# One core, two layers: the even layer's output projection in one pass over eight depth blocks, with the gated unit's results kept in DRAM

## The chip, the cores and the metric

One core of a Trainium2 chip runs the whole program. The time is device microseconds from the start to the end of one execution; three executions of the kernel before were timed, and one more was profiled.

TensorE multiplies (PE in the profile, its weight loads PEld), VectorE (DVE), ScalarE (ACT) and GpSimd (POOL) work on tiles, and SyncE (SP) issues every transfer of this kernel. TensorE's granted clock has two levels, 1.2 and 2.4 GHz; the profile's 1.00 is the higher.

## The reference, cut to what matters

2176 tokens (128 of a prompt, 2048 of a sample) of width 1024 in float32 pass two layers. The even layer has two branches of width 512 behind one input projection: a gated linear recurrence in two directions (o_a), and a state space model whose result passes a gated unit (o_b2). Both go through one output projection and are added to the residual. The odd layer is a gated short convolution with its own projections. What the change touches is this:

```python
    y = jax.nn.gelu(y.reshape(bsz, L, B_WIDTH))
    y = y * jax.nn.sigmoid(jnp.dot(y, w_glu) + b_glu)
...
    o_a = o.reshape(bsz, L, A_WIDTH) * jax.nn.silu(g_a)
...
    o_b2 = y_b * jax.nn.silu(g_b)
    out = jnp.dot(jnp.concatenate([o_a, o_b2], axis=-1).astype(h.dtype), w_out)
...
        yp = (yp.astype(F32) + g_p[:, None, :] * op.astype(F32)).astype(x_prompt.dtype)
        ys = (ys.astype(F32) + g_s[:, None, :] * os_.astype(F32)).astype(x_sample.dtype)
```

The depth of the output projection is 1024, which is eight blocks of 128: blocks 0 to 3 are o_a, blocks 4 to 7 are o_b2.

## The kernel before, in words

**Layout.** Features lie on the 128 partitions and tokens along them. The tokens are cut into six tiles (`TILES`): five of 384 and a last one, tile 5, of 256; `PARTS` makes pairs 0 (tiles 0, 1), 1 (2, 3) and 2 (4, 5). A float32 factor is split into hi and lo of type float32r, and a product is three matmuls, hi with hi, hi with lo, lo with hi (`mm3`, L356). A tile of activations split so is an `hhi` and an `hlo` of [128, 8, 384] from the pool `hp`, which has three slots for each of the two names.

**The order.** The tile framework orders the instructions of each engine ahead of time, by priority (in the main the order in which the program states them) and by its own model of time; on the chip each engine then runs its list in order, and waits where something is late. SP's list of transfers is such a list too: a transfer that waits holds up those behind it.

**The stages around the change.** First come the input projections, the scan of the state space model (its gelu results go to `y_d`) and the forward scan of the recurrence (`hgrn_run`), all interleaved. Gates go to DRAM as `zga` and `zgb`. Then:

- `bwd_chunk` (L891) does the backward scan, one chunk of 128 tokens after the other from chunk 16 down to 0. It loads `op_d`, `zga`, `qb_d` and `kv_d` (256 KB each), adds the backward part, normalises (a root on ScalarE, L922), transposes and stores 256 KB of o_a to `o_d` (L931). Chunks 16 to 12 are pair 2's tokens.
- `glu` (L949) works on a pair. It loads y into an `hlo` slot (L960), makes hi and lo copies for each tile in an `hhi` slot (L970, L971), and for each of four blocks does 12 matmuls (L979), a sigmoid out of PSUM (L983), the product with the gate `zgb` on GpSimd (L984), that with y on VectorE (L985), and a split into hi and lo (L986). y is stored with the 8 phases of a token group apart, so L970, L971 and L985 read it element by element. The results of the two tiles lie packed in one `hhi` and one `hlo` slot.
- `out_second` (L1000) multiplies these, blocks 4 to 7, by their half of the weights, 12 matmuls per output block and tile, and adds the result to x on VectorE (`evac_out`, L996). For pairs 0 and 1 the half-finished residual is stored to `x_d` (L1013); pair 2's stays in SBUF.
- The main loop then takes the pairs 2, 1, 0, with the later tile of each first (5, 4, then 3, 2, then 1, 0). `out_pair` with l = 0 multiplies blocks 0 to 3, which `load_o` (L1283) has read from `o_d` and split, by the other half of the weights, four output blocks at a time (`OUTE`), and adds; squares are summed on the way for the norm. Then come the backward chunks of the next pair, the odd layer's input projection and convolution (`in_odd`), the loads for the next pair, and `out_pair` with l = 1, two output blocks at a time, whose end normalises and stores the output.

**Buffers.** `big` is one slot of [128, 8, 384] that raw loads of `load_o` and the second tile's convolution results share. `xr` has three slots for residuals, `zg` four for the gates, `st` four for sigmoids. PSUM gives the gated unit two banks for matmul results, and the main loop five. Weights (512 KB a load) are split by ScalarE (L342) and by VectorE or GpSimd in turn (L346).

## Time and profile before

| | us |
|---|---|
| median of three runs | 2485.75 |
| lowest and highest | 2468.01, 2489.28 |
| the profiled execution | 2480.67 |
| its span, first to last instruction | 2478.9 |

The profile is of one execution. Busy time is the time in which an engine has an instruction; matmuls overlap each other, so the mean of one (some 330 ns) is longer than its share of the time. Idle time before an instruction is put down to what released it last. In the windows PEclk is the mean granted clock, DMA the mean busy share of 16 transfer engines; it can pass 1 a little where transfers overlap the edge of a window.

### The profile page before, as it was taken

What the parts mean: (1) busy time and instruction counts of PE and PEld (TensorE: products, weight loads), DVE (VectorE), ACT (ScalarE), POOL (GpSimd) and SP (SyncE); (2) the same over time, 40 slices, a digit from 0 to 9 for tenths busy, and PEclk for the clock granted to TensorE, in tenths of its full rate; (3) what the DMA queues carried; (4) which work ended last, traced back from release to release, by engine and by line L of the source; (5) the groups of instructions that cost most, each with busy time, mean ns of one, the idle gap of its engine ahead of it and who ended that gap; (6) DMA issues with size and microseconds to landing.
All of it is one profiled execution on the core that took longest, in us unless ns stands there. A gap on an engine that the chain in (4) does not pass through costs nothing. (4 is left out here: it accounts for less than half of the span.)

```text
span 2478.9 us, 46614 instructions
## 1 busy us (share of the span) xinstructions
PE 2320.4 (94%) x18452; PEld 2224.6 (90%) x18452; DVE 1381.5 (56%) x2960; ACT 988.5 (40%) x1989; POOL 678.1 (27%) x740
## 2 busy tenths in 40 slices
PE   5999889999999889998988899999999999999997
PEld 3999788988988779987988899999999999899997
DVE  5976879755557883366777632255622245522233
ACT  3544322334466774465444332233422232422231
POOL 0233431323223233233122222223222222322221
PEclk8999989999999899999998999999999999999999
DMA  7576643555575474554876332234221224122121
GB/s 261 148 221 198 195 138 101 152 149 149 150 219 161 133 220 133 170 160 126 295 252 213 111 95 76 77 102 158 72 64 60 68 78 139 57 64 65 60 68 60
DMA packets 277418, 335.96 MB, mean 136 GB/s; under 512 B 79056, under 2 KB 221136, under 8 KB 277072
## 3 DMA queue, kind: packets, MB, share of 16 engines
q1 hardware_dynamic: 277200, 332.99, 43.4%
q8 instruction: 145, 2.38, 0.4%
q14 instruction: 73, 0.60, 0.1%
HBM read 260.98 MB, written 71.94 MB: 134 GB/s over the span
## 5 line engine op out<-in xcount | busy, mean ns | idle before, releaser
L362 PE MATMUL pj<-hhi,whi 128*128 128x384 f32 (+1 forms) x3648 | 1173.5, 332 | 43.3 <-ACT hhi L304 25.9
L362 PE MATMUL pj<-hlo,whi 128*128 128x384 f32 (+1 forms) x3648 | 1174.9, 331 | 7.5 <-DVE hlo L305 5.8
L362 PE MATMUL pj<-hhi,wlo 128*128 128x384 f32 (+1 forms) x3456 | 1139.8, 330 | 0.1
L362 PEld LDWEIGHTS pj<-hhi,whi 128*128 128x128 f32 x3648 | 688.3, 190 | 55.0 <-ACT hhi L304 27.8
L362 PEld LDWEIGHTS pj<-hlo,whi 128*128 128x128 f32 x3648 | 688.4, 190 | 13.8 <-DVE hlo L305 8.5
L362 PEld LDWEIGHTS pj<-hhi,wlo 128*128 128x128 f32 x3456 | 657.9, 190 | 1.8 <-POOL wlo L346 0.6
L346 POOL TENSOR_TENSOR wlo<-wraw,whi 128x256 fp32r<-128x256 f32 x472 | 378.2, 832 | 1013.3 <-ACT whi L342 971.5
L342 ACT ACTIVATE whi<-wraw 128x512 fp32r<-128x512 f32 x472 | 271.7, 623 | 563.9 <-PE pj L362 358.1
L346 DVE TENSOR_TENSOR wlo<-wraw,whi 128x256 fp32r<-128x256 f32 x472 | 186.2, 452 | 114.2 <-ACT whi L342 113.3
L1056 DVE TENSOR_TENSOR ccg<-ccg,pj 128x384 f32<-128x384 f32 (+1 forms) x48 | 25.5, 531 | 248.2 <-PE pj L362 232.5
L829 POOL TENSOR_TENSOR hK<-hK,ht 128x512 f32<-128x512 f32 x68 | 93.3, 1373 | 242.7 <-ACT hMg L813 160.0
L996 DVE SCALAR_TENSOR_TENSOR xr<-pj,mod,xr 128x384 f32<-128x384 f32 (+2 forms) x152 | 77.4, 530 | 135.3 <-PE pj L362 123.2
L304 ACT ACTIVATE hhi<-nsq,mod 128x384 fp32r<-128x384 f32 (+2 forms) x144 | 74.3, 557 | 56.0 <-DVE nsq L302 55.9
L831 DVE TENSOR_TENSOR hQ<-hQ,ht 128x512 f32<-128x512 f32 x102 | 82.5, 822 | 15.4 <-PE lv L799 11.4
L283 DVE TENSOR_TENSOR nac<-nac,nsq 128x384 f32<-128x384 f32 (+1 forms) x112 | 72.3, 646 | 29.5 <-ACT nsq L282 27.4
L305 DVE SCALAR_TENSOR_TENSOR hlo<-nsq,mod,hhi 128x384 fp32r<-128x384 f32 (+2 forms) x144 | 82.0, 597 | 2.6 <-ACT hhi L304 2.6
L282 ACT ACTIVATE nsq<-xr 128x384 f32<-128x384 f32 (+1 forms) x84 | 42.0, 503 | 97.1 <-DVE xr L996 92.0
L1076 DVE TENSOR_TENSOR ccs<-ccs,pj 128x384 f32<-128x384 f32 (+1 forms) x48 | 25.3, 527 | 89.2 <-ACT ccs L1075 89.2
L572 POOL TENSOR_TENSOR SOt<-C,L 128x544 f32<-128x544 f32 x32 | 38.0, 1186 | 121.9 <-DVE SO L573 117.3
L979 PE MATMUL pj<-hhi 128*128 128x384 f32 (+1 forms) x192 | 54.0, 358 | 18.3 <-ACT hhi L970 12.2
L813 ACT ACTIVATE hMg<-hK 128x512 f32<-128x512 f32 x85 | 55.3, 653 | 37.2 <-PE lv L799 23.9
L1071 DVE TENSOR_TENSOR cca<-cca,pj 128x384 f32<-128x384 f32 (+1 forms) x48 | 25.4, 529 | 79.9 <-PE pj L362 79.7
(299 smaller groups left out, 2831.0 us busy)
## 6 DMA issues: line engine op xcount, KB each, us to landing
wraw<-in_w_in_odd SPq DMA_DIRECT2D x96, 512.0 KB
wraw<-in_w_in_even SPq DMA_DIRECT2D x92, 512.0 KB
mwm<-in_w_mod SPq DMA_DIRECT2D x64, 256.0 KB
big<-in_x SPq DMA_DIRECT2D x10, 1536.0 KB
wraw<-in_w_out_even SPq DMA_DIRECT2D x24, 512.0 KB
wraw<-in_w_out_odd SPq DMA_DIRECT2D x24, 512.0 KB
su<-u_d SPq DMA_DIRECT2D x64, 136.0 KB
pe<-et_d SPq DMA_DIRECT2D x32, 256.0 KB
```

The source lines that it names most:

```text
L282: nc.scalar.activation(sq[:, :n], x, AF.Square)
L283: e.tensor_tensor(acc, acc, sq[:, :n], op=OP.add)
L304: A.activation(hi[:, k, a:b], raw[:, a:b], AF.Identity, bias=sh)
L305: V.scalar_tensor_tensor(lo[:, k, a:b], raw[:, a:b], sh, hi[:, k, a:b].bitcast(F32), op0=OP.add, op1=OP.subtract)
L342: nc.scalar.activation(hi[:, i:i + ca], raw[:, i:i + ca], AF.Copy)
L346: e.tensor_tensor(lo[:, k], raw[:, k], hi[:, k].bitcast(F32), op=OP.subtract)
L362: nc.tensor.matmul(out=P[:, :n], lhsT=a[:, k, :], rhs=b[:, k, :n], start=(k == 0 and i == 0), stop=(k == kd - 1 and i == 2))
L813: A.activation(vw(Mg, 0, [(h, 2), (2 * h, nb), (1, h)]), vw(KK, 0, sp), AF.Copy)
L829: (G if lvl in KPOOL else V).tensor_tensor(kv, kv, vw(tot, n + 1, [(-n - 1, 2), (2, nb), (0, h)]), op=OP.mult)
L831: V.tensor_tensor(qv, qv, vw(tot, 1, [(n - 1, 2), (2, nb), (0, h)]), op=OP.mult)
L979: T.matmul(out=P[:, :n], lhsT=w[:, k, b * 128:b * 128 + 128], rhs=x[:, :n], start=(k == 0 and j == 0), stop=(k == 3 and j == 2))
L996: nc.vector.scalar_tensor_tensor(x[:, a:e], P[:, a:e], g.mod[l][:, 16 + b, s:s + 1], x[:, a:e], op0=OP.mult, op1=OP.add)
```

## The change

- `glu` no longer splits its results and no longer returns them. It takes y in the order in which it is stored, so that L970, L971 and L985 run over whole runs; matmuls and sigmoid see the tokens in that order. The product with y comes first, on VectorE; GpSimd then multiplies into the gate's tile `zgb`, reading the sigmoid's tile element by element to restore the order of the tokens, and that tile is stored to blocks 4 to 7 of `o_d`, which grows from four to eight blocks.
- `out_second`, `load_halves` and `x_d` are gone. The three pairs' gated units stand one after the other.
- `load_o` takes one tile, all eight blocks in one transfer into `big`, and splits it into its own `hhi` and `hlo`. For the first pair both tiles and x are loaded right behind the gated units. In the loop the next pair's first tile is loaded ahead of `out_pair` with l = 1, and its second tile behind it.
- `out_pair` treats both layers alike: eight depth blocks, 24 matmuls per output block and tile, two output blocks at a time (`OUTN`).
- x is read from the input for every pair.

```diff
--- before.py
+++ after.py
@@ -34,7 +34,6 @@
 EPS = 1e-6
 MAGIC = 12582912.0
 NQ = 2
-ORD2 = (0, 1, 2)
 NZG = 4
 RI = 500
 XP = 8
@@ -44,8 +43,7 @@
 AH = 1
 RS = 0
 GB = 8
-OUTE = 4
-OUTO = 2
+OUTN = 2
 NMD = 8
 MWB = 3
 RX = 0
@@ -345,12 +343,6 @@
         k = slice(i, i + cl)
         e.tensor_tensor(lo[:, k], raw[:, k], hi[:, k].bitcast(F32), op=OP.subtract)
     return hi, lo
-
-
-def load_halves(nc, g, src):
-
-    w = load_w(nc, g, src.rearrange("b p k m -> p b k m"))
-    return [tuple(t[:, 4 * i:4 * i + 4] for t in w) for i in range(2)]
 
 
 def mm3(nc, P, n, w, h):
@@ -959,17 +951,15 @@
             c0 = NSAM if s == 0 else (a - SEQ) // 8
             nc.sync.dma_start(rw[:, b, :, o:o + m], g.y_d[b * 128:b * 128 + 128, :, c0:c0 + m])
             o += m
-    out = {}
-    for i, ti in enumerate(pair):
+    for ti in pair:
         n = TILES[ti][1] - TILES[ti][0]
         m, c0 = n // 8, (TILES[ti][0] - t0) // 8
         hl = g.hp.tile([128, KD, 384], F32R, name="hhi")
-        ys = [vw(rw, b * 8 * mc + c0, [(1, m), (mc, 8)]) for b in range(4)]
+        ys = [vw(rw, b * 8 * mc + c0, [(mc, 8), (1, m)]) for b in range(4)]
         for b in range(4):
-            h = vw(hl, b * 384, [(8, m), (1, 8)])
+            h = vw(hl, b * 384, [(m, 8), (1, m)])
             A.activation(h, ys[b], AF.Copy)
-            V.tensor_tensor(vw(hl, (4 + b) * 384, [(8, m), (1, 8)]), ys[b], h.bitcast(F32), op=OP.subtract)
-        ob = g.hp.tile([128, KD, 384], F32R, name=("hhi", "hlo")[i])
+            V.tensor_tensor(vw(hl, (4 + b) * 384, [(m, 8), (1, m)]), ys[b], h.bitcast(F32), op=OP.subtract)
         for b in range(4):
             gb = g.zg.tile([128, 384], F32, name="zgb")
             nc.sync.dma_start(gb[:, :n], g.zgb[b, :, TILES[ti][0]:TILES[ti][1]])
@@ -981,11 +971,10 @@
             sg = g.st.tile([128, 384], F32, name="zst")
             b0 = PV["bglu"][0] + b
             A.activation(sg[:, :n], P[:, :n], AF.Sigmoid, bias=g.pv[:, b0:b0 + 1])
-            G.tensor_tensor(sg[:, :n], sg[:, :n], gb[:, :n], op=OP.mult)
-            V.tensor_tensor(vw(sg, 0, [(8, m), (1, 8)]), vw(sg, 0, [(8, m), (1, 8)]), ys[b], op=OP.mult)
-            split(nc, ob[:, b, :n], ob[:, 4 + b, :n], sg[:, :n])
-        out[ti] = ob[:, 0:4], ob[:, 4:8]
-    return out
+            V.tensor_tensor(vw(sg, 0, [(m, 8), (1, m)]), vw(sg, 0, [(m, 8), (1, m)]), ys[b], op=OP.mult)
+            gv = vw(gb, 0, [(8, m), (1, 8)])
+            G.tensor_tensor(gv, gv, vw(sg, 0, [(1, m), (m, 8)]), op=OP.mult)
+            nc.sync.dma_start(g.o_d[4 + b, :, TILES[ti][0]:TILES[ti][1]], gb[:, :n])
 
 
 
@@ -997,33 +986,13 @@
                                        op0=OP.mult, op1=OP.add)
 
 
-def out_second(nc, g, tiles, hs, xs, store):
-
-    for b in range(KD):
-        if b % 2 == 0:
-            ws = load_halves(nc, g, g.I["w_out_even"][b:b + 2, :, 4:8])
-        w = ws[b % 2]
-        for ti in tiles:
-            t0, t1 = TILES[ti]
-            n = t1 - t0
-            P = next(g.ps_p).tile([128, 512], F32, name="pj")
-            mm3(nc, P, n, w, hs[ti])
-            evac_out(nc, g, 0, ti, b, P, xs[ti][:, b])
-            if store and b % 2:
-                nc.sync.dma_start(g.x_d[(b - 1) * 128:b * 128 + 128, t0:t1].rearrange("(k p) t -> p k t", p=128),
-                                  xs[ti][:, b - 1:b + 1])
-
-
 def out_pair(nc, g, l, tiles, hs, xs, done):
 
     acc = {ti: g.nr.tile([128, 384], F32, name="nac") for ti in tiles}
-    m = (OUTE, OUTO)[l]
-    for b0 in range(0, KD, m):
-        b1 = b0 + m
-        if l == 0:
-            ws = [w for b in range(b0, b1, 2) for w in load_halves(nc, g, g.I["w_out_even"][b:b + 2, :, 0:4])]
-        else:
-            ws = [load_w(nc, g, g.I["w_out_odd"][b]) for b in range(b0, b1)]
+    w_out = g.I[("w_out_even", "w_out_odd")[l]]
+    for b0 in range(0, KD, OUTN):
+        b1 = b0 + OUTN
+        ws = [load_w(nc, g, w_out[b]) for b in range(b0, b1)]
         for ti in tiles:
             n = TILES[ti][1] - TILES[ti][0]
             for b, w in zip(range(b0, b1), ws):
@@ -1100,8 +1069,7 @@
     for nm in ("zq", "zff", "zfb", "zv", "zga", "zgb"):
         setattr(g, nm, dram(nm, [4, 128, NTOK]))
     g.op_d = dram("op_d", [NCH, 128, 512])
-    g.o_d = dram("o_d", [4, 128, NTOK])
-    g.x_d = dram("x_d", [D, NTOK])
+    g.o_d = dram("o_d", [8, 128, NTOK])
     g.h_d = dram("h_d", [6, 128, 2, KD, 384])
     g.u_d = dram("u_d", [512, 8, NC8])
     g.y_d = dram("y_d", [512, 8, NC8])
@@ -1280,25 +1248,18 @@
                     Sb = bwd_chunk(nc, g, c, Sb)
             return Sb
 
-        def load_o(pair):
-            raw = big(g)
-            os = {}
-            for i, ti in enumerate(pair):
-                t0, t1 = TILES[ti]
-                n = t1 - t0
-                r = raw[:, 4 * i:4 * i + 4, :n]
-                nc.sync.dma_start(r, g.o_d[:, :, t0:t1].rearrange("h p t -> p h t"))
-                o = g.hp.tile([128, KD, 384], F32R, name=("hhi", "hlo")[i])
-                for k in range(4):
-                    split(nc, o[:, k, :n], o[:, 4 + k, :n], r[:, k])
-                os[ti] = o[:, 0:4], o[:, 4:8]
-            return os
+        def load_o(ti):
+            t0, t1 = TILES[ti]
+            n = t1 - t0
+            r = big(g)[:, :, :n]
+            nc.sync.dma_start(r, g.o_d[:, :, t0:t1].rearrange("h p t -> p h t"))
+            return split_tile(nc, g, r, n)
 
         def xr():
             return g.xr.tile([128, KD, 384], F32, name="xr")
 
-        def load_xs(pair, src, rooms=None):
-            return {ti: load_x(nc, g, ti, src, rooms[i] if rooms else xr()) for i, ti in enumerate(pair)}
+        def load_xs(pair):
+            return {ti: load_x(nc, g, ti, I["x"], xr()) for ti in pair}
 
         def norm_odd(ti, sq):
             n = TILES[ti][1] - TILES[ti][0]
@@ -1320,13 +1281,11 @@
         order = [p[::-1] for p in (p2, p1, p0)]
         Sb = bwd(p2, Sb)
         with tc.tile_pool(name="zg", bufs=NZG) as g.zg:
-            for pair in ORD2:
-                obs = glu(nc, g, PARTS[pair], wg)
-                last = pair == 2
-                xs = load_xs(PARTS[pair], I["x"], None if last else (xr(), big(g)))
-                out_second(nc, g, PARTS[pair], obs, xs, not last)
+            for pair in PARTS:
+                glu(nc, g, pair, wg)
         g.ps_p, g.wp = itertools.cycle((ps_q, ps_p, ps_q, ps_p, ps_q)), itertools.cycle(((wp2, wp), (wp, wp), (wp, wp)))
-        os = load_o(order[0])
+        os = {ti: load_o(ti) for ti in order[0]}
+        xs = load_xs(order[0])
         for i, pair in enumerate(order):
             ta, tb = pair
             nxt = order[i + 1] if i < 2 else None
@@ -1348,9 +1307,11 @@
             nb = TILES[tb][1] - TILES[tb][0]
             ys = {ta: ya, tb: split_tile(nc, g, yb[:, :, :nb], nb)}
             if nxt:
-                os, xn = load_o(nxt), load_xs(nxt, g.x_d)
+                os = {nxt[0]: load_o(nxt[0])}
+                xn = load_xs(nxt)
             out_pair(nc, g, 1, pair, ys, xs, finish)
             if nxt:
+                os[nxt[1]] = load_o(nxt[1])
                 xs = xn
 
 
```

## Rows read from the trace of the kernel before

**Rows 1.** The page: span, busy time, share of the chain by engine.

```profile
span 2478.9 us, 46614 instructions
...
PE 2320.4 (94%) x18452; PEld 2224.6 (90%) x18452; DVE 1381.5 (56%) x2960; ACT 988.5 (40%) x1989; POOL 678.1 (27%) x740
...
PE 46%; DVE 2%; ACT 1%; issue 0%; POOL 0%; DVEq 0%; POOLq 0%; ACTq 0%
```

**Rows 2.** Windows: start:end, length, busy us (count) PE PEld DVE ACT POOL, PEclk, DMA, GB/s.

```profile
1418.00:1690.00 272.00, 272.00 (x1854) 271.96 (x1855) 103.97 (x225) 86.19 (x171) 70.55 (x92) 1.00 0.28 86
```

**Rows 3.** Windows, columns as above: the touched stretch, cut by stage.

```profile
1158.50:1199.00 40.50, 31.21 (x262) 27.34 (x248) 23.32 (x42) 23.14 (x43) 8.90 (x10) 0.92 0.68 190
1199.00:1236.70 37.70, 36.86 (x216) 35.89 (x217) 26.08 (x55) 12.58 (x18) 4.87 (x6) 1.00 1.06 346
1236.70:1265.00 28.30, 22.32 (x111) 20.62 (x110) 20.36 (x30) 14.99 (x24) 11.92 (x11) 0.88 0.80 276
1265.00:1302.00 37.00, 36.45 (x220) 36.03 (x219) 26.87 (x55) 11.65 (x20) 5.59 (x5) 1.00 0.81 244
1302.00:1325.40 23.40, 19.55 (x120) 19.03 (x119) 16.26 (x32) 14.57 (x25) 8.43 (x11) 0.85 0.97 311
1325.40:1391.00 65.60, 62.49 (x417) 61.32 (x415) 41.92 (x91) 25.32 (x50) 19.29 (x25) 0.95 0.42 133
```

**Rows 4.** Windows of rows 3, projection matmuls (L362) alone: PE and PEld.

```profile
1199.00:1236.70 37.70, 34.75 (x192) 33.08 (x192) 1.00 1.06 346
...
1265.00:1302.00 37.00, 34.40 (x192) 32.87 (x191) 1.00 0.81 244
```

**Rows 5.** Groups by line, 1158.5:1391: form, count, busy, mean ns, idle before and releaser.

```profile
L979 PE MATMUL pj<-hhi 128*128 128x384 f32 (+1 forms) x192 | 54.0, 358 | 18.3 <-ACT hhi L970 12.2 <-ACT zst L983 4.7 <-DVE hhi L971 1.2
...
L996 DVE SCALAR_TENSOR_TENSOR xr<-pj,mod,xr 128x256 f32<-128x256 f32 (+2 forms) x54 | 26.9, 516 | 27.6 <-PE pj L362 27.1
...
L984 POOL TENSOR_TENSOR zst<-zst,zgb 128x384 f32<-128x384 f32 (+1 forms) x24 | 24.6, 1036 | 63.4 <-ACT zst L983 28.1 <-DVE wlo L346 17.0 <-issue 9.7
...
L985 DVE TENSOR_TENSOR zst<-zst,hlo 128x384 f32<-128x384 f32 (+1 forms) x24 | 22.3, 935 | 12.4 <-POOL zst L984 12.4
L971 DVE TENSOR_TENSOR hhi<-hlo,hhi 128x384 fp32r<-128x384 f32 (+1 forms) x24 | 20.4, 876 | 11.0 <-ACT hhi L970 11.0
...
L970 ACT ACTIVATE hhi<-hlo 128x384 fp32r<-128x384 f32 (+1 forms) x24 | 19.1, 842 | 11.8 <-DMA hlo<-y_d 11.8
...
L983 ACT ACTIVATE zst<-pj,pv 128x384 f32<-128x384 f32 (+1 forms) x24 | 13.1, 561 | 19.7 <-PE pj L979 19.4
...
L922 ACT ACT_TABLE_LOAD x7 | 9.0, 1283 | 0.1
```

**Rows 6.** Timeline of ACT, first uses of two loads.

```profile
1164.35 0.85 ACT L970 ACTIVATE hhi<-hlo 128x384 fp32r<-128x384 f32 x1 [6.44 <-DMA hlo<-y_d]
...
1649.17 1.77 ACT L311 ACTIVATE hhi<-big 128x384 fp32r<-128x384 f32 x4 [3.40 <-DMA big<-o_d]
```

**Rows 7.** Timeline of SP's DMA issues: start, length of the issue, line, tiles, count.

```profile
1159.10 1.27 SPq L960 DMA_DIRECT2D hlo<-y_d  x2
...
1295.55 0.36 SPq L931 DMA_DIRECT2D o_d<-bo  x1
...
1345.72 0.37 SPq L931 DMA_DIRECT2D o_d<-bo  x1
...
1348.11 0.33 SPq L897 DMA_DIRECT2D bo<-op_d  x1
...
1643.93 0.93 SPq L1290 DMA_DIRECT2D big<-o_d  x2
```

**Rows 8.** Timeline of PE: start, length, instruction, [idle before and releaser].

```profile
1246.64 0.62 PE L979 MATMUL pj<-hhi 128*128 128x384 f32 x2 [1.44 <-ACT hhi L970]
...
1256.46 1.01 PE L979 MATMUL pj<-hhi 128*128 128x384 f32 x2 [3.98 <-ACT zst L983]
...
1315.01 0.80 PE L979 MATMUL pj<-hhi 128*128 128x256 f32 x2 [3.46 <-ACT hhi L970]
```

## Prediction

> **What bounds the kernel now.** I read the page first: TensorE is busy for 2320.4 of 2478.9 us, and of the chain that ended last, as far as it was followed, TensorE holds 46 of 49 hundredths [rows 1]. So a change that leaves TensorE's instructions alone can give or take only the time in which TensorE idles or runs at its lower clock, and I looked for that time stage by stage. Behind the touched stretch there is next to none: 272 us of the odd layer are 272.00 us busy at granted clock 1.00 [rows 2]. The touched stretch is 1158.5 to 1391 us, and the table of windows [rows 3] holds the whole argument: gated unit of pair 0 with the tail of the forward scan; second half of its projection; the same two for pair 1; gated unit of pair 2; then pair 2's second half and first half together. Idle time is length less PE busy: 9.3, 0.8, 6.0, 0.6, 3.9 and 3.1, together 23.6 us. A stretch at mean clock c has lost (1 - c) of its length, since the low level is half the high one (1.2 against 2.4 GHz): 3.2, 0, 3.4, 0, 3.5, 3.3, together 13.4 us. Before, then, 37.0 of these 232.5 us are lost, and 195.5 are work. The reader should see that the loss sits in the gated unit, not in the projection: the two stretches that are mostly projection lose 1.4 us in 74.7.
>
> **What is moved at no price.** The projection multiplies as before: 24 matmuls per output block and tile, now in one accumulation instead of 12 and 12. 192 matmuls (pair 0) take 34.75 us and pair 1's 34.40 [rows 4]. These 69 us leave the stretch and come back as longer projections of pairs 1 and 0, where TensorE has weights ready in the same rhythm: by the loops one weight load still serves 48 matmuls, 24 loads before and 24 after. So the sum is: new time = old time + (loss after - 37.0).
>
> Also costed at nothing: 56 residual updates (L996, half a microsecond each [rows 5]) go, VectorE being 104 us busy in those 272 [rows 2]; 12.6 MB of residuals (4 tiles of 1.57 MB, stored and reloaded) go, 8.9 MB of gated results written and read come, in stretches where DMA has a share of 0.28 [rows 2]. The splits into hi and lo stay 48 in number; those of the gated half move from the gated unit to the load of the projection's input. For later pairs these lie under the odd projection (about 69 us for two tiles at the pace of [rows 4]): the first tile's load follows the last use of the one raw buffer, the second tile's splits wait for the slot that the odd projection's first tile frees, and have its last 48 matmuls and then the next tile's 48, 8.7 us each, against 8 splits at 0.44 us (four in 1.77 [rows 6]) and as many subtractions. Waiting for that slot, they hold up ScalarE's queue (squares, weight splits), which has this much slack. Were that cover gone, each of two pairs would lose some 5 us.
>
> **Loss after, term by term.**
> (a) The start of the first gated unit: 9.3 + 3.2 = 12.5 us now, mostly a wait for y (issued 1159.10, first copy 1164.35, matmul later [rows 6, 7]). The copies L970 and subtractions L971 now read and write runs instead of single elements; the row for contiguous copies is 0.44 us [rows 6] against 0.84 and 0.88 [rows 5]. I take 11.
>
> (b) Gated units 2 and 3 lose 9.8 + 6.9 = 16.7 us now. Two of their waits are for L970 of a pair's second tile, 1.44 and 3.46 us [rows 8]: of three slots for hi one holds the gate's weights, one the first tile's copies, one its results, so the second tile's copies wait until the first tile's matmuls end. The change takes the results out of these slots. That returns 4.9 us and one fall of the clock, 3.5. The other wait, 3.98 us for the sigmoid [rows 8], comes from a backward scan chunk on ScalarE: its root needs another table than the sigmoid, 1.28 us each way [rows 5], while two PSUM buffers hold 4.2 us of matmuls. Three gated units now run without a projection between them, so the five chunks of pair 2 fall into them: I add 2.7. Sum 11, bounds 4 (no chunk hurts) and 20 (every chunk costs 4).
> By the Trainium skill (page ScalarE: Activation LUTs, section Table sets: the hidden batching unit) alternating functions of two sets costs a load of about 2.7 us each time; the row has 1.28, and the row decides. By the page's price three chunks would add 8.5 us more and the forecast would be 2503.
>
> (c) The pace inside. Per block: 12 matmuls 2.1 us, sigmoid 0.56, VectorE product under 0.94, GpSimd product 1.04 [rows 5]; so TensorE leads if buffers return in time. The GpSimd product now reads single elements, which no row shows; between 1.04 and 2.0 (stretched as ScalarE's copies, 0.84 to 0.44) it stays below 2.1, and I take 1.04. But a gate buffer now lives from its load through the product until its store has landed: 5.2 us (a load under traffic [rows 6, 7]) + 1.0 + 2.4 (a store of 256 KB until its buffer was loaded again, 1345.72 to 1348.11 [rows 7]) = 8.6, over four buffers 2.15 us a block, level with TensorE. Behind each store, which waits on SP's queue for GpSimd, stand the next gate load and the scan's loads and stores. And DMA: y, gates and results 4.46 MB each, five chunks 6.6, x of pair 2 2.6, weights and the scan's tail 3.4, some 26 MB, take 75 us at the 346 GB/s of a full window [rows 3], of the 91 us that there are (work of the three gated windows 63, and 28 of (a) to (c)). I take 6, bounds 0 and 23 (3.05 us a block: load and store 5.2 each, two issues of 0.4).
>
> (d) A new gap: the last gated tile (tile 5) is the first that the projection reads. Sigmoid 0.5, VectorE 0.5, GpSimd 0.8, store issue 0.4, store 2.4, load of 1 MB 6.0 (5.2 us for 0.75 MB beside as much again, 1643.93 to 1649.17 [rows 6, 7]), first split 0.4: 11.0 us, in which TensorE has nothing but scan pieces of about 1 us; behind the waiting load on SP's queue stand tile 4's load, x and weights. One fall of the clock, 3.4 as in [rows 3]. Together 14.4; bound below 10.
> By the Trainium skill (page DMA: Bandwidth & Descriptors, section Anatomy of one DMA) a transfer costs 2.0 us plus its bytes at 436 GB/s, so each hop through DRAM pays that twice: an estimate of 6.7 us for hop and return, against my 8.4 from rows; by it the forecast would be 2492. The page fitted it on GpSimd's queue, which no run here uses.
>
> (e) Tile 4's load waits for the raw buffer, which tile 5's eight splits and subtractions hold for 4.2 us; then 7.0 us for 1.5 MB (the 5.2 above, and 0.75 MB more at 346 GB/s, less its overlap) and 1.0 for the first split. Tile 5's first two blocks, 48 matmuls of 256 columns, end about 7.9 us after its data landed, so 4.3 us of idling and 2.7 of clock: 7.0, bounds 3 and, with the next rival, far more.
>
> (f) 1 us inside pair 2's projection, instead of 3.1 + 3.3: its splits and updates no longer crowd in behind the gated unit.
>
> Loss after: 11 + 11 + 6 + 14.4 + 7 + 1 = 50.4, against 37.0: 13.4 us slower, 0.5%. The sum stands on the profiled execution, 2480.67 us (span 2478.9); the median of the runs, 2485.75, is 5 us above it and the lowest 12.7 below, so about 1% is what a measurement here can tell from no change.
>
> **Rivals.**
> The scan comes last (slower). Tile 4 needs chunks 14 to 12. Before, chunk 12's store was issued at 1295.55 [rows 7], and nothing needed it early, since projections ran in between. If scan and gated unit go on delaying each other on ScalarE and VectorE, and that time stays, tile 4's data land 2.4 + 6.6 us later and its matmuls start at about 1306; with 51.7 us of projection left (336 matmuls at the pace of [rows 4], two thirds of it for 256 columns), 7 of scan pieces and 3.4 of clock, pair 2 ends at 1368 instead of 1336: 32 us more, 2526. For it: they meet on ScalarE, and one such meeting held TensorE for 3.98 us [rows 8]. Against it: 12.6 MB of x and residuals leave these windows, and 4.46 MB of results come. It decides once chunk 12's store is issued after 1262 (1249.5, the gated units' end by (a) to (c), and 4.6 + 6.0 + 4.6 less 2.4), and costs 1% in all when it comes after 1273.
>
> The gated unit is paced by its gate buffers (slower): (c) at 23 instead of 6 gives 2511.
>
> The freed slots are worth it (faster, within 1%): (a) 9.5, (b) 4, (c) 0, (d) 10, (e) 3, (f) 1 = 27.5, so 9.5 us gained, 2471. More than that would need the loss below 12, less than (a) and the 10 of (d) together.
>
> **How the numbers follow.** Forecast 0.50, scan last 0.20, gate buffers 0.15, freed slots 0.15. The forecast's time is 2494. The range, 2471 to 2526, goes from the freed slots to the scan. Faster by over 1%: 0.03, since no case gets there. Slower by over 1%: the scan 0.20, half of the gate buffers 0.08, a tail of the forecast 0.03: 0.31. Within 1%: 0.66.
>
> **What would show it.** Right: no L362 row between the gated units; the L970 waits of second tiles gone; behind the last L979 an idle gap of 10 to 12 us ended by a split of tile 5's load, then one of some 4 us for tile 4; the windows behind as full as before. Wrong in (c): L979 waiting for the sigmoid, and that for a buffer or a store on the DMA queue. Scan last: the second gap over 15 us, ended by a load issued right behind a scan store. Wrong altogether: idle time in the odd layer, or in the projections of pairs 1 and 0, which I cost at nothing.

## The result, and the profile after

The changed kernel takes 2494.07 us (median of 20 runs), the kernel before beside it 2481.07 us (20 runs): a ratio of 1.0055, 95% interval 1.0041 to 1.0069. It is slower by half a per cent, which stays within the 1% that the forecast called no change; the forecast was 2494.0 us. The profiled execution has a span of 2491.6 us, 12.7 more than before.

The page of the changed kernel: span, busy time, share of the chain by engine.

```profile
span 2491.6 us, 46534 instructions
...
PE 2322.3 (93%) x18452; PEld 2229.8 (89%) x18452; DVE 1338.4 (54%) x2904; ACT 976.7 (39%) x1987; POOL 685.1 (27%) x740
...
PE 69%; DMA 11%; DVE 10%; ACT 3%; issue 3%; SPq 2%; POOL 1%; DVEq 0%; ACTq 0%; POOLq 0%
```

TensorE still runs 18452 matmuls and is busy for about as long (2322.3 against 2320.4 us [rows 1]), so the 12.7 us are, but for some 2, idle time. Line numbers of after: gated unit copies L961 and subtractions L962, gate load L965, matmuls L969, sigmoid L973, VectorE product L974, GpSimd product L976, gated store L977; backward scan L889 to L923 (its PE steps L903 and L921, its store L923); load of the stacked results L1255 with splits L309 and L310; projection matmul L354.

Windows of after: start:end, length, busy us (count) of PE, PEld, DVE, ACT, POOL, granted clock, DMA share, GB/s. The rows are two for the gated units, the gap before tile 5, tile 5's first blocks, the rest of pair 2's projection, the odd layer.

```profile
1160.90:1202.00 41.10, 35.82 (x293) 33.98 (x286) 23.07 (x45) 20.41 (x45) 12.96 (x10) 0.96 0.91 245
1202.00:1243.50 41.50, 32.71 (x193) 30.61 (x191) 27.67 (x58) 21.95 (x35) 12.62 (x10) 0.88 0.96 317
1243.50:1268.40 24.90, 7.69 (x37) 6.42 (x37) 10.66 (x23) 5.09 (x10) 5.77 (x6) 0.58 0.93 285
1268.40:1280.60 12.20, 8.77 (x61) 8.48 (x61) 9.72 (x26) 4.95 (x14) 0.72 (x1) 0.88 0.75 232
1280.60:1333.40 52.80, 52.80 (x342) 52.77 (x343) 17.14 (x36) 16.43 (x36) 21.13 (x27) 0.97 0.26 76
...
1360.00:1640.00 280.00, 280.00 (x1895) 279.97 (x1895) 104.56 (x231) 91.55 (x181) 72.67 (x96) 1.00 0.29 90
```

Read the idle time as in [rows 3]: 5.3, 8.8, 17.2, 3.4 and 0 us. Half of it stands in one place, the 24.9 us between the last gated matmul and the first projection matmul; there TensorE does 7.69 us of scan pieces, at a mean clock of 0.58. The odd layer behind is as full as before [rows 2].

Where the 12.7 us are: the stretch from 1158.5 to 1391 was 232.5 us long, of which 69.15 us of matmuls left [rows 4], so 163.35 remained; after, it is 1160.9 to 1333.3, 172.4 us: 9.05 more. Another 2.4 had been lost before it starts. What comes behind grew from 1087.9 to 1158.3 us, by 70.4, which is the 69.15 moved and 1.25 more.

The timeline around the gap: start, length, engine, line, and in brackets the idle time ahead and what ended it. First GpSimd's last products, then SyncE's issues, on ScalarE a sigmoid and the first split, and PE, with its last gated matmul.

```profile
1249.52 0.85 POOL L976 TENSOR_TENSOR zgb<-zgb,zst 128x256 f32<-128x256 f32 x1 [0.28 <-DMA zgb<-zgb]
1251.83 0.85 POOL L976 TENSOR_TENSOR zgb<-zgb,zst 128x256 f32<-128x256 f32 x1 [1.46 <-DMA zgb<-zgb]
1255.84 0.85 POOL L976 TENSOR_TENSOR zgb<-zgb,zst 128x256 f32<-128x256 f32 x1 [3.16 <-DVE bo L922]
1257.54 0.85 POOL L976 TENSOR_TENSOR zgb<-zgb,zst 128x256 f32<-128x256 f32 x1 [0.84 <-DMA zgb<-zgb]
...
1255.76 0.37 SPq L923 DMA_DIRECT2D o_d<-bo  x1
...
1258.41 0.32 SPq L977 DMA_DIRECT2D o_d<-zgb  x1
...
1260.89 0.37 SPq L1255 DMA_DIRECT2D big<-o_d  x1
...
1272.82 0.37 SPq L1255 DMA_DIRECT2D big<-o_d  x1
...
1247.67 0.47 ACT L973 ACTIVATE zst<-pj,pv 128x256 f32<-128x256 f32 x1 [3.53 <-POOL zgb L976]
...
1267.92 2.56 ACT L309 ACTIVATE hhi<-big 128x256 fp32r<-128x256 f32 x8 [5.97 <-DMA big<-o_d]
...
1243.15 0.28 PE L969 MATMUL pj<-hhi,hlo 128*128 128x256 f32 x1
...
1253.92 1.09 PE L921 MATMUL ax<-eye,bsq 128*128 128x128 f32 x4 [7.85 <-DVE bsq L916]
1257.20 2.05 PE L903 MATMUL ax<-hS,bq 128*128 128x128 f32 x8 [2.19 <-DMA bq<-qb_d]
1263.03 1.08 PE L921 MATMUL ax<-eye,bsq 128*128 128x128 f32 x4 [3.78 <-DVE bsq L916]
1268.39 0.80 PE L354 MATMUL pj<-hhi,whi 128*128 128x256 f32 x2 [2.57 <-ACT hhi L309]
...
1280.57 0.75 PE L354 MATMUL pj<-hhi,whi 128*128 128x384 f32 x3 [3.43 <-ACT hhi L309]
```

TensorE's last gated matmul ends at 1243.4. The four products of tile 5 then come as late as 1257.54, waiting for gate loads and for VectorE, whose queue holds scan steps ahead of the products; the third block's sigmoid, too, waits 3.5 us for GpSimd to give back one of the four sigmoid buffers. The last gated store is issued at 1258.41, 15.0 us after the matmul. The load follows 2.5 us later (SyncE issues two loads of the scan in between, and then waits 0.7 us for the store), its data are split 7.0 us after that, and 0.5 us later TensorE starts: 25.0 us. Chunk 12's scan store, which tile 4 needs, is issued at 1255.76, only 2.65 us before the last gated store; tile 4's own load, at 1272.82, goes out as soon as tile 5's splits leave the raw buffer (1272.79). Note also what the idle time of PE is put down to: mostly to the scan's transposes, since TensorE runs its instructions in the order written, and these stand ahead of the projection.

So the trace leaves two theories (and more). **Theory 1:** the hop from the gated products through DRAM into tile 5 is the loss. **Theory 2:** the backward scan, a chain of five chunks that can't start before the forward scan ends, would hold the projection as long. **Theory 3:** four gate buffers make the products late. After the first four runs came **theory 4**, hop and scan lie side by side and either is long enough to hide what the other costs, and its rival **theory 5**, the loss is the work of the stretch or lies elsewhere; for the kernels that give hop and scan a cover, theory 5 says that the second load and split of the weights takes it back.

### The profile page after: what moved, and what is told of

Same layout as the page of the kernel before. It is cut to its first block, busy times and chain, and to the rows that moved or that the text cites. A ratio compares the mean times of both kernels' runs of the same rounds, so it can differ in the third digit from the quotient of the medians.

```text
span 2491.6 us, 46534 instructions
## 1 busy us (share of the span) xinstructions
PE 2322.3 (93%) x18452; PEld 2229.8 (89%) x18452; DVE 1338.4 (54%) x2904; ACT 976.7 (39%) x1987; POOL 685.1 (27%) x740
## 4 chain that ended last, share of the span: by engine, by line
PE 69%; DMA 11%; DVE 10%; ACT 3%; issue 3%; SPq 2%; POOL 1%; DVEq 0%; ACTq 0%; POOLq 0%
PE pj L354 61%; DMA pe<-et_d 2%; DMA wraw<-in_w_in_even 1%; DMA gs_d<-GS 1%; DVE hlo L303 1%; DMA mwm<-in_w_mod 1%; DVE scv L658 1%; PE lv L791 1%; DVE nsq L300 1%; PE ax L865 1%; DVE wlo L344 1%; DMA sM<-gs_d 1%; PE lv L717 1%; DMA hff<-zff 1%; PE nx L224 1%
## 5 line engine op out<-in xcount | busy, mean ns | idle before, releaser
L354 PE MATMUL pj<-hhi,whi 128*128 128x384 f32 (+1 forms) x3648 | 1207.8, 333 | 44.3 <-ACT hhi L302 22.1
L354 PE MATMUL pj<-hlo,whi 128*128 128x384 f32 (+1 forms) x3648 | 1208.6, 332 | 8.3 <-DVE hlo L303 8.3
L354 PE MATMUL pj<-hhi,wlo 128*128 128x384 f32 (+1 forms) x3648 | 1206.3, 331 | 0.1
L354 PEld LDWEIGHTS pj<-hhi,whi 128*128 128x128 f32 x3648 | 696.6, 191 | 55.0 <-ACT hhi L302 23.6
L354 PEld LDWEIGHTS pj<-hlo,whi 128*128 128x128 f32 x3648 | 696.2, 191 | 14.1 <-DVE hlo L303 11.0
L354 PEld LDWEIGHTS pj<-hhi,wlo 128*128 128x128 f32 x3648 | 696.7, 191 | 2.3 <-DVE wlo L344 0.6
L340 ACT ACTIVATE whi<-wraw 128x512 fp32r<-128x512 f32 x472 | 271.7, 623 | 556.9 <-PE pj L354 369.7
L985 DVE SCALAR_TENSOR_TENSOR xr<-pj,mod,xr 128x384 f32<-128x384 f32 (+2 forms) x112 | 58.9, 539 | 184.4 <-PE pj L354 176.7
L302 ACT ACTIVATE hhi<-nsq,mod 128x384 fp32r<-128x384 f32 (+2 forms) x144 | 74.1, 558 | 52.6 <-DVE nsq L300 52.4
L823 DVE TENSOR_TENSOR hQ<-hQ,ht 128x512 f32<-128x512 f32 x102 | 82.6, 823 | 14.9 <-PE lv L791 11.0
L303 DVE SCALAR_TENSOR_TENSOR hlo<-nsq,mod,hhi 128x384 fp32r<-128x384 f32 (+2 forms) x144 | 84.3, 613 | 1.7 <-ACT hhi L302 1.7
L281 POOL TENSOR_TENSOR nac<-nac,nsq 128x384 f32<-128x384 f32 (+1 forms) x42 | 42.9, 1022 | 143.3 <-ACT nsq L280 143.0
L384 ACT ACTIVATE zst<-pj 128x384 f32<-128x384 f32 (+1 forms) x96 | 44.5, 464 | 66.9 <-issue 34.1
```

What stands on the lines that cost most here:

```text
L281: e.tensor_tensor(acc, acc, sq[:, :n], op=OP.add)
L302: A.activation(hi[:, k, a:b], raw[:, a:b], AF.Identity, bias=sh)
L303: V.scalar_tensor_tensor(lo[:, k, a:b], raw[:, a:b], sh, hi[:, k, a:b].bitcast(F32), op0=OP.add, op1=OP.subtract)
L340: nc.scalar.activation(hi[:, i:i + ca], raw[:, i:i + ca], AF.Copy)
L354: nc.tensor.matmul(out=P[:, :n], lhsT=a[:, k, :], rhs=b[:, k, :n], start=(k == 0 and i == 0), stop=(k == kd - 1 and i == 2))
L384: nc.scalar.activation(st[:, :n], P[:, :n], AF.Copy)
```

## The experiments

Each ratio is to the kernel before on the same chip; an expected time is to be read beside the 2481.07 us of the kernel before, so a ratio of 1.0034 stands for 2489.5 us. The "stretch" of a kernel is measured in its profile from the beginning of the wait for the first gated copy (PE free) to the end of the last of pair 2's 384 even projection matmuls; in after it is 1161.5 to 1333.4. What is left from there to the end of the span is the last column.

| kernel | ratio, interval | stretch us | PE idle in it us | behind it us |
|---|---|---|---|---|
| after | 1.0055 (1.0041 to 1.0069) | 171.9 | 34.7 | 1158.2 |
| e_nogate | 1.0034 (1.0018 to 1.0049) | 162.9 | 29.4 | 1162.3 |
| e_noscan | 1.0034 (1.0017 to 1.0051) | 164.1 | 29.3 | 1160.0 |
| e_late | 1.0001 (0.9983 to 1.0020) | 164.2 | 27.1 | 1150.8 |
| e_late_nogate | 0.9942 (0.9920 to 0.9964) | 138.7 | 14.9 | 1164.2 |
| e_zg12 | 1.0035 (1.0019 to 1.0051) | 175.5 | 36.5 | 1152.0 |
| e_bq2 | 1.0022 (1.0007 to 1.0036) | 173.8 | 38.9 | 1150.9 |
| e_oldlay | 1.0046 (1.0027 to 1.0066) | 174.8 | 33.0 | 1152.1 |
| e_order | 1.0027 (1.0012 to 1.0043) | 170.2 | 33.6 | 1152.9 |
| e_order_bq2 | 1.0016 (1.0002 to 1.0030) | 171.4 | 39.0 | 1151.4 |
| e_tile | 1.0016 (0.9994 to 1.0037) | 165.7 | 28.5 | 1152.5 |
| e_tile_zg12 | 1.0013 (0.9997 to 1.0029) | 164.9 | 24.3 | 1150.9 |
| e_tile_bq2 | 1.0000 (0.9987 to 1.0013) | 164.3 | 30.1 | 1149.6 |

A stretch is that of one execution, a ratio that of 6 to 20 runs; the start of the stretch differs by up to 11.6 us between the profiles (1160.6 to 1172.2), so lengths are compared and not ends. What lies behind differs as well, by up to 14.6 us, mostly at the odd norm right behind the stretch and at the next pair's, though most of these edits lie ahead of it; so what a kernel gains is read from its ratio, and the stretch says where. Each edit also lets the tile framework order the instructions anew, so none changes one thing alone. 0.001 of the ratio is 2.5 us.

### Taking the two waits away, one by one and together

**e_nogate** loads blocks 4 to 7 of pair 2 from data that were there all along:

```diff
-            nc.sync.dma_start(r, g.o_d[:, :, t0:t1].rearrange("h p t -> p h t"))
+            first = ti in order[0]
+            for j, src in enumerate((g.o_d[0:4], g.zgb if first else g.o_d[4:8])):
+                nc.sync.dma_start(r[:, 4 * j:4 * j + 4], src[:, :, t0:t1].rearrange("h p t -> p h t"))
```

> The changed kernel, but the loads of the first pair's stacked results take blocks 4 to 7 from the raw gate tensor instead of the gated results, in a transfer of their own, so nothing waits for the gated stores (the output of tokens 1536 on is not the reference's: that part is left out). Theory 1 (the exposed hop from the gated products through DRAM is the loss): the 24.9 us between the last gated matmul (1243.4) and the first projection matmul of tile 5 (1268.4) shrinks to under 10, the time falls by 12 to 20 us against the changed kernel, to 2474 to 2482. Theory 2 (the backward scan's last chunk, stored at 1255.8, holds the projection as much): tile 5 starts early, PE then waits before tile 4, for the store of chunk 12, its landing and a 7 us load; the time falls by 0 to 8 us, to 2486 to 2494.

Measured: 1.0034, some 5 us less than after; the stretch is 9.0 us shorter, and what lies behind it 4.1 us longer. Its timeline behind tile 5's first blocks, SyncE, ScalarE and PE:

```profile
1268.32 0.37 SPq L923 DMA_DIRECT2D o_d<-bo  x1
...
1270.80 0.37 SPq L1257 DMA_DIRECT2D big<-o_d  x1
...
1277.45 1.77 ACT L309 ACTIVATE hhi<-big 128x384 fp32r<-128x384 f32 x4 [5.48 <-DMA big<-o_d]
...
1278.03 0.74 PE L354 MATMUL pj<-hhi,whi 128*128 128x384 f32 x3 [2.17 <-ACT hhi L309]
```

Tile 5's projection starts among the last gated matmuls (1251 us). But then TensorE waits, first in the scan's transposes (5.1 and 3.8 us), and tile 4 starts 9.7 us after chunk 12's store, by the same hop: store, load, split. This is theory 2's picture, and the 5 us lie in the range that it gave (0 to 8 less).

**e_noscan** does the same with blocks 0 to 3 (source `g.zga if first else g.o_d[0:4]`).

> The changed kernel, but the first pair's loads take blocks 0 to 3 from the raw gate tensor of the scan instead of the scan's results, in a transfer of their own, so nothing there waits for the scan (the output of tokens 1536 on is not the reference's: that part is left out). Theory 1 (gated hop): the first projection matmul still starts about 25 us after the last gated matmul, the time stays within 4 us of the changed kernel, 2490 to 2496. Theory 2 (the scan's last chunk): the time falls by 6 us or more, to 2488 or less.

Measured: 1.0034, stretch 7.8 us shorter. It is neither theory's number (2490 to 2496, 2488 or less). The scan's steps still stand in TensorE's order ahead of tile 4, with waits of 4.5, 1.6, 3.8 and 0.8 us; only the data no longer matter.

**e_late** also puts the five chunks behind the projection in the program:

```diff
-        Sb = bwd(p2, Sb)
         with tc.tile_pool(name="zg", bufs=NZG) as g.zg:
...
             out_pair(nc, g, 0, pair, os, xs, norm_odd)
+            if i == 0:
+                Sb = bwd(p2, Sb)
```

> The changed kernel with pair 2's five backward-scan chunks put behind its projection, whose loads take blocks 0 to 3 from the scan's raw gate tensor (the output of tokens 1536 on is not the reference's: the scan's part of it is left out there); the wait for the gated stores stays. Theory 1 (the gated hop alone): PE still stands about 20 us between the last gated matmul and tile 5, and the ratio to the kernel before stays at 1.003 to 1.0055. Theory 4 (hop and scan run side by side, and either alone is long enough): the same, the ratio falls by no more than 0.002. Theory 2 (scan alone): the ratio falls by 0.005 or more, below 1.001.

**e_late_nogate** is e_late with blocks 4 to 7 from `g.zgb` too.

> As e_late, and blocks 4 to 7 are loaded from the raw gate tensor too, so the first projection waits for neither the scan nor the gated stores (the output of tokens 1536 on is not the reference's: both parts are left out there). Theory 4 (hop and scan hide each other): PE goes from the last gated matmul to tile 5 in under 3 us, the 17 to 20 us of idle and the low clock that follows go, the ratio to the kernel before falls to 0.993 to 0.998. Theory 5 (the loss is elsewhere: the stretch's total work on ACT, VectorE and GpSimd, or later stages): the ratio stays above 1.001.

The stretch in one row (columns as above), for after, e_late and e_late_nogate:

```profile
1161.50:1333.40 171.90, 137.18 (x911) 131.85 (x911) 87.65 (x183) 68.83 (x137) 53.20 (x53) 0.88 0.71 216
```

```profile
1164.80:1329.00 164.20, 137.12 (x899) 132.73 (x899) 88.36 (x174) 65.49 (x133) 53.35 (x53) 0.91 0.72 217
```

```profile
1160.60:1299.30 138.70, 123.78 (x855) 120.61 (x855) 73.47 (x139) 61.85 (x125) 55.85 (x53) 0.95 0.74 224
```

e_late comes out at 1.0001, 13 us less than after by the ratios, 7.7 by the stretch and 7.4 behind it. A fall of 0.0054 to 1.0001 is theory 2's number; theory 4 had allowed 0.002. But the hop is still there, as theories 1 and 4 said: the first projection matmul that needs a gated result starts at 1270.73, 16.7 us after the last gated matmul. And the scan is not gone: the framework still puts five chunks ahead of it, and in the stretch TensorE waits 11.0 us for scan transposes. The fifth scan store and the load of tile 4's gated half, in e_late:

```profile
1266.47 0.46 SPq L923 DMA_DIRECT2D o_d<-bo  x1
...
1272.58 0.51 SPq L1257 DMA_DIRECT2D big<-o_d  x1
```

e_late_nogate comes out at 0.9942, 28 us less than after; its stretch is 33.2 us shorter, of which 6.0 come back behind it, and TensorE's waits for the splits of tiles 5 and 4 are down to four of 0.5 to 0.9 us:

```profile
PE pj L354 <- DVE hlo L310: 1.6, 2, 0.9
PE pj L354 <- ACT hhi L309: 1.0, 2, 0.5
```

What follows: by the ratios the hop's data are worth 5 us, the scan's data and its place in the program 13, both together 28. Stretch and what lies behind it, added up, say the same of one execution each: 4.9, 15.1 and 27.2 us. (The stretch alone would give 9.0, 7.7 and 33.2.) Neither theory 1 nor theory 2 alone can give that: with the scan moved, the hop still costs 15 us, and with the hop gone, the scan 23.

Together the two are worth 9 us more than one by one, 0.0038 of the ratio, which is hardly more than its uncertainty (0.0036, an estimate from the four intervals). So they overlap in part, as theory 4 says in kind; that either alone hides the other, its strong form, is not borne out. Theory 5 as it was put (a ratio above 1.001) is excluded: the same work takes 28 us less.

What is not separated: how much of this is the wait for data, how much the place of the scan's steps in TensorE's order, and how much their work on VectorE and ScalarE. In the stretch of after eight chunks run (VectorE adds their result, L904, eight times), in that of e_late seven, in that of e_late_nogate three; the others then run beside later matmuls. In each of these kernels the load of one transfer became two, half a tile each, so a projection could start on its first four blocks; what that alone is worth was not measured.

### Buffers

**e_zg12**: the gate blocks live in the three residual tiles, idle there, four each.

```diff
+        gr = g.xr.tile([128, KD, 384], F32, name="xr")
         for b in range(4):
-            gb = g.zg.tile([128, 384], F32, name="zgb")
+            gb = gr[:, b]
```

> The changed kernel with twelve gate buffers (four for each of three large tiles, which stand idle there) in place of four; nothing left out. Theory 3 (the gated products lag because a gate buffer comes free only when its store has landed): the last gated store moves from 15.0 us after the last gated matmul to about 5, and the time falls by 8 to 12 us, to 2482 to 2486. Theory 1 without theory 3 (the hop is store, load and split, the products' lag is ACT, VectorE and GpSimd work): the last gated store moves by under 4 us, the time is 2490 to 2494.

Its gated stores, one row: count, durations, first and last start.

```profile
L978 SPq DMA_DIRECT2D o_d<-xr x24: 319/320/1061, 1207.2 to 1261.0; - x24
```

The last gated matmul ends at 1256.25, so the last store is 4.7 us behind it and not 15.0: the lag was the four buffers, as theory 3 says. Yet the ratio is 1.0035, 5 us less where 8 to 12 were expected, and in its profile that stands behind the stretch, which is 3.6 us longer. The lag was shortened, but the gated units took about as much longer: their matmuls end 91.7 us after the start of the stretch, in after 81.9. TensorE waits for the scan among them (3.1 and 5.3 us at 1199 and 1206) and again behind them, in four pieces of 11.0 us together, of which the longest is

```profile
1268.56 1.09 PE L921 MATMUL ax<-eye,bsq 128*128 128x128 f32 x4 [4.87 <-DVE bsq L916]
```

From the last gated matmul to the first projection matmul it is still 18.2 us, where after has 25.0.

**e_bq2**: e_zg12 with a second buffer for the scan's query block (`bufs=1` taken away).

> The changed kernel with twelve gate buffers (as in e_zg12) and two buffers in place of one for the scan's query block (bq); nothing left out. Theory 4 (the scan's five chunks are a chain of some 11 us each, and the query block's load, for whose buffer the chunk before must be done, is a part of each): the chunks come 1 to 2 us closer, the last store 5 to 8 us earlier, the ratio to the kernel before is 1.000 to 1.003. Rival (the chain is the arithmetic between PE, ACT and VectorE): the last chunk's store does not move, the ratio stays at 1.0035.

Measured: 1.0022. The five scan stores come at 1215.1, 1230.4, 1238.5, 1256.9 and 1262.9, 47.8 us from first to last, against 52.0 in e_zg12 (1209.6 to 1261.6) and 42.3 in after. But that is because the first ones come later: counted from the start of the stretch, the first store is issued after 49.7 us here and 45.0 in e_zg12, the last after 97.5 and 97.0. That is what the rival said of the store. The ratio lies in theory 4's range, but its difference from e_zg12 is within both intervals.

### The token order in the gated unit

**e_oldlay** undoes the order of the copies alone:

```diff
-        ys = [vw(rw, b * 8 * mc + c0, [(mc, 8), (1, m)]) for b in range(4)]
+        ys = [vw(rw, b * 8 * mc + c0, [(1, m), (mc, 8)]) for b in range(4)]
...
-            gv = vw(gb, 0, [(8, m), (1, 8)])
-            G.tensor_tensor(gv, gv, vw(sg, 0, [(1, m), (m, 8)]), op=OP.mult)
+            G.tensor_tensor(gb[:, :n], gb[:, :n], sg[:, :n], op=OP.mult)
```

(and the three views of the copies, subtractions and VectorE products with it).

> The changed kernel with the token order of before inside the gated unit (the high and low parts written with a stride of 8 elements, the products on VectorE strided, GpSimd's product contiguous); nothing left out. Theory of the prediction (the contiguous order is worth a shorter start, 2.6 us, and shorter copies that lie beside PE): the ratio to the kernel before rises by 0 to 0.003 over the changed kernel's 1.0055. Rival (the gated products bound the hop and GpSimd's single-element read makes them late): the ratio falls by 0.001 to 0.002.

Groups by line over the stretch, after, then e_oldlay: count, busy us, mean ns, idle time ahead and its releasers.

```profile
L976 POOL TENSOR_TENSOR zgb<-zgb,zst 128x384 f32<-128x384 f32 (+1 forms) x24 | 29.8, 1253 | 50.6 <-DVE brc L913 13.1 <-DMA zgb<-zgb 11.2 <-DVE zst L974 8.8
...
L962 DVE TENSOR_TENSOR hhi<-hlo,hhi 128x384 fp32r<-128x384 f32 (+1 forms) x24 | 15.3, 686 | 6.0 <-ACT hhi L961 5.9
L974 DVE TENSOR_TENSOR zst<-zst,hlo 128x384 f32<-128x384 f32 (+1 forms) x24 | 14.6, 618 | 12.9 <-ACT zst L973 12.9
...
L961 ACT ACTIVATE hhi<-hlo 128x384 fp32r<-128x384 f32 (+1 forms) x24 | 10.5, 496 | 6.3 <-DMA hlo<-y_d 6.3
L914 ACT ACT_TABLE_LOAD x5 | 6.4, 1283 | 0.1
```

```profile
L974 DVE TENSOR_TENSOR zst<-zst,hlo 128x384 f32<-128x384 f32 (+1 forms) x24 | 22.1, 943 | 9.7 <-ACT zst L973 9.7
L962 DVE TENSOR_TENSOR hhi<-hlo,hhi 128x384 fp32r<-128x384 f32 (+1 forms) x24 | 20.5, 902 | 6.5 <-ACT hhi L961 6.5
L961 ACT ACTIVATE hhi<-hlo 128x384 fp32r<-128x384 f32 (+1 forms) x24 | 19.1, 854 | 5.9 <-DMA hlo<-y_d 5.8
```

The contiguous order takes 8.6 us from ScalarE and 12.7 from VectorE (15.3 + 14.6 against 20.5 + 22.1). The ratio with the old order is 1.0046, within the interval of after: these instructions lie beside other work, and neither side's sign is shown. The stretch is 174.8 us against 171.9, but what lies behind it is 6.1 us shorter, so that decides nothing either.

### Giving the hop and the scan a cover

**e_order** runs the gated units in the order pair 2, 1, 0 (`for pair in PARTS[::-1]`), so that pair 2's results are long in DRAM when its projection starts.

> The changed kernel with the gated units in the order pair 2, 1, 0, so that pair 2's gated results are stored some 60 us before its projection starts; nothing left out. Theory 1 (gated hop): the load of tile 5 waits only for its buffer, PE goes from the last gated matmul to tile 5 in under 8 us, the time falls by 12 to 20 us, to 2474 to 2482. Theory 2 (the scan's last chunk holds the pair): PE waits before tile 4 instead, the time falls by 0 to 8 us, to 2486 to 2494.

Its waits of PE over the stretch: total us, times, longest us.

```profile
PE ax L921 <- DVE bsq L916: 12.8, 4, 6.0
PE pj L969 <- ACT zst L973: 10.4, 3, 9.1
PE pj L354 <- ACT hhi L309: 5.1, 2, 2.9
PE pj L969 <- ACT hhi L961: 4.9, 2, 4.3
```

The hop is covered: tile 5's load is issued at 1242.85, in the middle of the gated units, and its projection waits 2.2 us. But the scan's waits stay (6.0 and 3.8 us, then 2.9 for tile 4's split), and a new one of 9.1 us stands ahead of a gated matmul, for a sigmoid whose output buffers wait for products and these for gate loads. 1.0027 is theory 2's number, and the wait before tile 4 is the one it named.

**e_tile** adds tile 5's whole projection ahead of tile 4's, so that it covers the scan's last chunks; pair 2's weights are then loaded and split twice.

```diff
-            out_pair(nc, g, 0, pair, os, xs, norm_odd)
+            for part in ([ta], [tb]) if i == 0 else (pair,):
+                out_pair(nc, g, 0, part, os, xs, norm_odd)
```

> The changed kernel with the gated units in the order pair 2, 1, 0, and pair 2's even projection done for all eight output blocks of tile 5 and then for tile 4 (its weights are loaded twice); nothing left out. Theory 4: the gated hop is hidden behind pairs 1 and 0, the scan's last chunks behind tile 5's some 20 us of matmuls; the ratio to the kernel before falls to 0.995 to 1.000. Theory 5: the extra 4 MB of weights and their splitting cost what the cover gives, the ratio stays at 1.002 or above.

**e_tile_zg12** has the twelve gate buffers too, **e_tile_bq2** the second query buffer on top, and **e_order_bq2** both buffers without the projection by tiles.

> e_tile (gated order pair 2, 1, 0; pair 2's projection tile by tile) with twelve gate buffers; nothing left out. If the 8.9 us in which PE waited there for a sigmoid behind a late gate load is due to four gate buffers, it goes, and the ratio to the kernel before falls from 1.0016 to 0.998 or below; if it is due to the length of SyncE's queue, the ratio stays within 0.001 of e_tile's.

> e_tile_zg12 with two buffers for the scan's query block; nothing left out. Theory 4: the scan's last chunk falls behind tile 5's matmuls altogether, PE's idle time between 1160 and 1335 falls from some 25 us to under 15, the ratio to the kernel before is 0.994 to 0.998. Theory 5 (the second load and split of the weights takes it back): 1.000 to 1.003.

> e_tile_bq2 without the tile-by-tile projection (weights loaded once): gated order pair 2, 1, 0, twelve gate buffers, two buffers for the scan's query block; nothing left out. Theory 4: tile 4's wait for the scan's last chunk stays, so it gets about half of what e_tile_bq2 gets, a ratio of 0.998 to 1.002. Theory 5: without the extra weights it is the faster of the two, 0.995 to 0.999.

Measured: 1.0016, 1.0013, 1.0000 and 1.0016. Only the last lies in theory 4's range. e_tile falls between the two ranges; e_tile_zg12 stays within 0.001 of e_tile, although the 8.9 us wait of e_tile went with the twelve buffers: it was due to the four, but its going gained nothing that could be measured; e_tile_bq2 lies at the edge of theory 5's range, and its idle time is 30.1 us, where theory 4 asked for under 15. The waits of PE over the stretch of e_tile_bq2:

```profile
PE pj L354 <- ACT whi L340: 9.3, 2, 7.2
PE ax L903 <- DMA bkv<-kv_d: 8.6, 1, 8.6
PE pj L970 <- ACT zst L974: 7.0, 3, 5.0
```

In e_tile the scan's share falls to 4.1 us (from 17.7 in after over 1160.9 to 1280.6), and in e_tile_bq2 nothing behind the gated units waits for a scan step. In its place 9.3 us go to the weights that are split a second time (ScalarE, L340), 8.6 to the scan's loads at its start, 7.0 to sigmoids. e_tile_bq2 is as fast as the kernel before and 0.5% faster than the changed one; e_order_bq2, without the projection by tiles, keeps a wait of 13.6 us for the scan and 5.9 for tile 4. So the cover that theory 4 asks for takes the scan's waits away, and, as theory 5 said, waits for the second weight split and others come in their place. No kernel that leaves nothing out is clearly faster than the kernel before.

## Why the prediction was right, and where it was not

**The method holds.** TensorE's work is the same, the odd layer is full, no L354 row stands among the gated units, and most of what changed is loss in one stretch. The forecast was 13.4 us, the measured medians are 13.0 apart; in the profile the stretch gave 9.05, the part ahead of it 2.4, the rest 1.25. The loss in the stretch after is 172.4 less 126.35 us of work (195.5 less 69.15), so 46.0, where the terms made 50.4. That the total came out to 0.1 us is luck: (a) to (c) were 7 us too large and (d) about as much too small, the 3.65 us outside the stretch had been put at nothing, and the sum stood on one execution of 2480.67 us, close to the later median of 2481.07; on the median of three runs known then, 2485.75, it would have been 2499.

**Terms (a) to (c)** were too large. By idle time and clock as in [rows 3], the first window lost 6.9 us (5.3 and 1.6) where (a) said 11; the second 13.8 (8.8 and 5.0) where (b) and (c) said 17. The waits for the second tile's copies of pairs 1 and 2 are gone, as (b) said; the meetings with the scan that (b) added are there, but as transposes and query loads that PE waits for, not as sigmoids (0.3 us in all). The gated matmuls ended at 1243.4, not 1249.5.

**The table loads.** (b) took 1.28 us from a row; the loads of after take 1283 ns each (five of them in the row of L914 above), and the next function follows at once: in after a sigmoid ends at 1234.91 and the root behind the load starts at 1236.22, 1.31 us later.

```profile
1234.33 0.58 ACT L973 ACTIVATE zst<-pj,pv 128x384 f32<-128x384 f32 x1 [0.35 <-POOL zgb L976]
1234.92 1.28 ACT L914 ACT_TABLE_LOAD   x1
1236.22 0.30 ACT L914 ACTIVATE brc<-brc,eps 128x4 f32<-128x4 f32 x1
```

So the 2.7 us that the Trainium skill gives for such a change (page ScalarE: Activation LUTs, section Table sets: the hidden batching unit) are not borne out here.

**Term (d), the hop, was too small by nearly half.** It said 11.0 us of idling and 3.4 of clock; there are 25.0 us, 17.2 of them idle, and the sign that it named, a gap of 10 to 12 us, did not come. The total held all the same; the step of (d) that failed is its first: sigmoid, two products and the store's issue were summed as 2.2 us, as if the last block were alone. (c) had worked out that a gate buffer returns only when its store has landed, and put the price on the pace of the matmuls; but here TensorE's matmuls ran ahead of the gates (0.3 us of waits for a sigmoid), so the price collected behind them, at the end, where it counted: 15.0 us to the last store, 4.7 with twelve buffers. That they run ahead is not sure: in e_order a gated matmul waited 9.1 us at the end of the same chain of buffers. The other pieces were close: store to load 2.5 (2.4 forecast), load 7.0 (6.0). By the fit in the Trainium skill (page DMA: Bandwidth & Descriptors, section Anatomy of one DMA), which is for GpSimd's queue, the estimate is 2.3 us for the 128 KB store and 4.4 for the 1 MB load; the store is near that, the load, on SyncE's queue and with DMA at a share of 0.93, is not.

**Term (e)**: 3.4 us of idling and 1.5 of clock, where it said 4.3 and 2.7. **Term (f)**: no idling and 1.6 of clock, where it said 1.

**A flaw of the sum.** Idle time and (1 - c) of a window count an idle stretch at low clock twice. In the window of the gap they give 17.2 + 10.5 us in 24.9, though the low clock can cost something only in the 7.69 us in which PE is busy, 3.8 at most. Taken over the five windows the sum is 54.8 so, and 48.1 with that one corrected, nearer to the 46.0 of the lengths. The 37.0 us of before were added up in the same way, so the 195.5 us of work and the 46.0 carry the flaw too.

**The rival "scan last"** was put as another outcome, from which the forecast is safe while chunk 12's store is issued before 1262. It was issued at 1255.76, so the rival did not come. But the runs show that this was no margin: without the hop, tile 4 hangs on that store (e_nogate), and with the scan's data and place changed the time falls by 13 us though the hop stays (e_late). The forecast priced the two as alternatives; both cost at once, 28 us of the time together, 5 and 13 singly.

**The rival "freed slots"** fails by (d), some 21 us where it needed 10, and by the second window, 13.8 where it needed 4. **"Gate buffers"** had the right cause at the wrong place, above.

**Costed at nothing, and not quite nothing.** Around the second pair's even projection TensorE lost more than before. Windows of before and of after:

```profile
1640.00:1780.00 140.00, 135.94 (x848) 134.83 (x847) 82.69 (x164) 55.32 (x108) 43.13 (x48) 0.99 0.39 125
```

```profile
1640.00:1780.00 140.00, 133.96 (x778) 132.64 (x778) 74.92 (x154) 47.00 (x88) 37.98 (x44) 0.96 0.42 132
```

2 us more of idling, and a clock of 0.96 in place of 0.99; the waits are for the odd norm (L302, L303), not for the load of the stacked results, which the prediction had named. Other places give most of it back, since all that lies behind the stretch has grown by only 1.25 us net. No run was made for this, and its cause stays open; but it comes and goes with the order ahead of it: in e_zg12, which changes nothing there, the 180 us around the same norm (from 300 us behind the end of the stretch) have 4.9 us of idling at a clock of 0.99, in after 6.0 at 0.97.

**Open too:** what splitting the load in two is worth by itself, and why the start of the stretch moved by up to 11.6 us between the profiles of kernels that differ only behind it.

## What to carry to other kernels

When work that ran between a producer and its consumer is moved elsewhere, ask what it was covering: here the projections between the gated units hid a trip through DRAM and a serial scan, and both came to light at once. Two such waits side by side are not alternatives to be priced one instead of the other: taking one away gave 5 or 13 us, taking both 28, so test them together as well. And read what an edit gains from the whole time: a stretch cut out of the profile showed 9, 8 and 33 us for the same three, because what lay behind the cut had changed as well. And a buffer that returns late need not slow the engine in front of it; look for its price at the end of the queue, in the time from the last matmul to the last store.

## What the runs showed of the hardware

- GpSimd's product that reads single elements takes 1253 ns on the mean, contiguous 1139 (e_oldlay) and 1036 in the kernel before; the two contiguous ones lie as far apart, so what single elements cost there is not known more closely than 100 to 200 ns. The same change of order takes ScalarE's copies from 854 to 496 ns and VectorE's products from 943 to 618.
- In the 24.9 us of the gap, with PE busy for 7.69 us, the mean granted clock was 0.58; over the whole stretch it was 0.88, and 0.95 where both waits were taken away (e_late_nogate).
- A transfer of 1 MB took 7.0 us from its issue to its first use with DMA at a share of 0.93, a store of 128 KB 2.5 us until the load that needs it was issued.
